# A transformer encoder layer on one core: the first sequence's output projection by seven products of block sums, in two halves of the depth, and its final norm beside the second sequence's products

## The chip, the cores and the metric

One core of one Trainium2 chip. The metric is the device time of one execution in microseconds, median of three runs. Engines: PE (TensorE, matmuls), PEld (its weight loads), DVE (VectorE), ACT (ScalarE), POOL (GpSimd) and SP (SyncE, which issues most DMAs).

## What is computed

One layer of a bidirectional encoder for a sample of 1024 tokens and a prompt of 512 tokens, D = 2048, in fp32, and a final norm:

```python
h = rms_norm(x, norm_g)
z = h @ w_in
c_val, c_glu, c_gate, q, k, v, a_gate = split(z)
conv_out = conformer_conv(c_val, c_glu, w_dw, b_dw, ln_g, ln_b, w_pw) * silu(c_gate)
attn_out = banded_sink_attention(rope(q), rope(k), v, sink) * silu(a_gate)
y = rms_norm(x + concat([conv_out, attn_out]) @ w_out, final_norm_g)
```

`conformer_conv` is a gated unit, a depthwise convolution of 31 taps, a layer norm over 1024 channels, a silu and a product with `w_pw` (1024 x 1024). The attention has 8 heads of 128 in two groups, in bands of blocks of 128 tokens. `w_out` is 2048 x 2048: its first 1024 rows meet the convolution half of the mix, its last 1024 the attention half. Weights are the same for both sequences.

## The kernel before

Every fp32 product is made as three products of parts: ACT copies a tile into its upper part (L379), DVE subtracts that from the tile and leaves the lower part (L380, `parts`), and PE multiplies upper by upper, upper by lower and lower by upper into one bank of PSUM. Matmuls have a 128x128 weight and 128x512 of tokens. Values lie channel by channel in partitions, tokens along the row; the first sequence has two halves of 512 tokens.

**Seven products.** The first sequence's input projection is made by units (`Unit`). A unit takes two columns of 128 outputs, the two halves of 512 tokens and 8 blocks of 128 of the depth (1024), and treats them as a 2x2 by 2x2 product of blocks: seven products of sums and differences of blocks instead of eight. Each is 4 blocks x 3 parts = 12 matmuls (L190), so a unit has 84. The weight differences are made on DVE from two raw tiles (L140, `make1` and `make2`), the sums of token blocks come from DRAM, where they were put earlier (`load_sum`, `token_sum`). `tap` (L216, L236) evacuates each product from PSUM and adds it to up to four results on ACT and DVE. The depth of 2048 takes two units; the first stores its part in DRAM, the second adds it by an accumulating DMA that POOL issues. Units of one half of the depth come one after the other; at the change to the other half (`switch`) the token sums are exchanged step by step.

**Jobs.** All other products are jobs (`Job`): one column of 128 outputs by 512 tokens. The prompt's input projection has jobs of 48 matmuls (L517), a job of `w_pw` 24, a job of `w_out` 48.

**Order of the work.** Python code emits everything in the order in which it shall run on PE; each engine runs its own rows in that order and waits for semaphores. First come the units of the first sequence's input projection (4 stages), then the prompt's jobs, then for each of three posts (the sample's two halves, `Post`, and the prompt, `LastPost`) eight `first_jobs` (with `w_pw`) and for the sample's halves sixteen `last_jobs` (with `w_out`), 2 x 16 x 48 matmuls in all. Beside these, lanes (`conv`, `attn`, `prep`) hand out side work step by step, as matmul time goes by (`tick`), at a rate set by `pace`: the convolution's taps, the attention, the norms. `until` forces a lane's steps out before the job that needs them. A post's layer norm (`prepare`) sums the channels on DVE (L1089, L1091) and over partitions on PE (L559), takes squares, the column sums (L548), a root, spreads it (L584) and makes the normed, silu'd tiles and their parts. The sample's second half has its norm beside the first half's `last_jobs` (it is started at `lj[1]`), and the prompt's beside the second half's. `project` adds the residual and gathers squares; `finish`, the final norm, scales 16 tiles of a half (L1192) and stores them.

**The end.** `last_run` makes the prompt's output projection with tokens in partitions: four blocks j of 512 output columns; in each, four accumulators (one for each 128 tokens) take 48 matmuls of 128x512 each (L1316). `rows_done` (L1287 and on) adds the residual rows (`x_p`), squares, and scales. `load_rows` (L1272, L1276) loads the final norm's gain and the rows of `x_p`, 512 KB each, ahead of the run. Accumulators alternate between two sets of four banks: a, b, a, c and s, s, pt, pv.

The functions that the change touches, and what calls them:

## Time and profile before

| | |
|---|---|
| median of three runs | 2159.8 us (2158.51 to 2161.04) |
| profiled execution, its own time | 2161.61 us |
| its span in the trace | 2159.8 us |
| granted TensorE clock, mean | 0.997 |
| PE busy | 2121.6 us, 98% |
| DVE busy | 1631.5 us, 76% |
| ACT busy | 1017.6 us, 47% |
| DMA | 400.13 MB, 185 GB/s |

A row of the trace's chain or timeline has the start in us from the span's start, the length, the engine, the source line (L517 is line 517 of the kernel before), and how often. In square brackets stands how long the engine was idle just before and what released it. A row of a group by line and form has `out<-in` by the program's names, the shape and type of both, the count, then busy us, mean ns of one, and the idle time before these with its releasers. A row of the windows has the stretch, its length, the busy time of PE, PEld, DVE, ACT and POOL with counts, the granted clock, the DMA share and GB/s.

### The profile page before, as it was taken

What the parts mean: (1) busy time and instruction counts of PE and PEld (TensorE: products, weight loads), DVE (VectorE), ACT (ScalarE), POOL (GpSimd) and SP (SyncE); (2) the same over time, 40 slices, a digit from 0 to 9 for tenths busy, and PEclk for the clock granted to TensorE, in tenths of its full rate; (3) what the DMA queues carried; (4) which work ended last, traced back from release to release, by engine and by line L of the source; (5) the groups of instructions that cost most, each with busy time, mean ns of one, the idle gap of its engine ahead of it and who ended that gap; (6) DMA issues with size and microseconds to landing.
All of it is one profiled execution on the core that took longest, in us unless ns stands there. A gap on an engine that the chain in (4) does not pass through costs nothing.

```text
span 2159.8 us, 26503 instructions
## 1 busy us (share of the span) xinstructions
PE 2121.6 (98%) x9510; PEld 1747.2 (81%) x9510; DVE 1631.5 (76%) x2493; ACT 1017.6 (47%) x1620; POOL 77.4 (4%) x92
## 2 busy tenths in 40 slices
PE   8999999999989999899999999999999999999998
PEld 5887888888878888688888888888888888888886
DVE  8657799988889999899887669986675467446343
ACT  6475445333544444544464656745574325232232
POOL 0001110000011111000000000000000000000000
PEclk9999999999999999999999999999999999999999
DMA  8978878754766767754446444564534493438342
GB/s 276 324 255 248 227 179 272 267 181 156 234 189 176 185 156 203 236 179 161 138 142 225 131 138 137 166 216 154 190 122 135 152 316 110 150 113 268 97 128 78
DMA packets 208037, 400.13 MB, mean 185 GB/s; under 512 B 18976, under 2 KB 76704, under 8 KB 207904
## 3 DMA queue, kind: packets, MB, share of 16 engines
q1 hardware_dynamic: 195232, 375.36, 52.5%
q0 software_dynamic: 12672, 23.07, 6.6%
q8 instruction: 74, 1.21, 0.2%
q14 instruction: 59, 0.48, 0.1%
HBM read 294.02 MB, written 104.33 MB: 184 GB/s over the span
## 4 chain that ended last, share of the span: by engine, by line
PE 79%; issue 9%; DVE 5%; DMA 3%; ACT 2%; POOL 2%; SPq 0%; POOLq 0%; ACTq 0%; DVEq 0%
PE a L517 21%; PE a L190 13%; PE c L517 11%; PE b L517 10%; PE c L190 6%; PE b L190 3%; PE s L971 2%; PE pv L1000 2%; PE a L1316 2%; PE s L1316 2%; PE pt L1005 1%; PE b L1316 1%; PE c L1316 1%; PE pv L1316 1%; PE pt L1316 1%
## 5 line engine op out<-in xcount | busy, mean ns | idle before, releaser
L379 ACT ACTIVATE hl<-raw 128x1024 fp32r<-128x1024 f32 (+1 forms) x332 | 312.8, 943 | 509.8 <-issue 109.0
L380 DVE TENSOR_TENSOR hl<-raw,hl 128x1024 fp32r<-128x1024 f32 (+1 forms) x332 | 357.7, 1078 | 250.9 <-ACT hl L379 246.0
L517 PE MATMUL a<-t,hl 128*128 128x512 f32 x2112 | 505.7, 392 | 1.2 <-DVE hl L380 1.2
L190 PE MATMUL a<-t,hl 128*128 128x512 f32 x1968 | 475.6, 392 | 13.7 <-ACT t L382 7.5
L517 PEld LDWEIGHTS a<-t,hl 128*128 128x128 f32 x2112 | 392.7, 188 | 81.6 <-DVE hl L380 1.7
L845 DVE SCALAR_TENSOR_TENSOR f<-f,c_w_dw,f 128x1024 f32<-128x1024 f32 (+1 forms) x464 | 454.2, 1013 | 3.6 <-ACT f L840 3.4
L190 PEld LDWEIGHTS a<-t,hl 128*128 128x128 f32 x1968 | 369.3, 189 | 96.7 <-ACT t L382 7.9
L517 PE MATMUL b<-t,hl 128*128 128x512 f32 x1056 | 253.9, 392 | 0.1
L517 PE MATMUL c<-t,hl 128*128 128x512 f32 x1056 | 253.2, 392 | 0.0
L190 PE MATMUL c<-t,hl 128*128 128x512 f32 x984 | 239.1, 390 | 3.1 <-ACT t L379 1.1
L517 PEld LDWEIGHTS b<-t,hl 128*128 128x128 f32 x1056 | 196.3, 188 | 40.3 <-DVE hl L380 0.6
L517 PEld LDWEIGHTS c<-t,hl 128*128 128x128 f32 x1056 | 196.6, 188 | 39.8
L190 PEld LDWEIGHTS c<-t,hl 128*128 128x128 f32 x984 | 184.4, 188 | 43.4 <-ACT t L379 2.2
L190 PE MATMUL b<-t,hl 128*128 128x512 f32 x492 | 118.6, 389 | 0.0
L190 PEld LDWEIGHTS b<-t,hl 128*128 128x128 f32 x492 | 92.3, 188 | 19.3
L216 ACT ACTIVATE g<-a 128x512 f32<-128x512 f32 x88 | 52.2, 593 | 67.2 <-PE a L190 60.6
L379 ACT ACTIVATE a<-pt 128x512 fp32r<-128x512 f32 x64 | 38.1, 596 | 79.1 <-PE pt L1005 78.9
L216 ACT ACTIVATE u<-a 128x512 f32<-128x512 f32 x76 | 45.3, 596 | 63.5 <-PE a L190 59.8
L1316 PE MATMUL a<-hl,t 128*128 128x512 f32 x192 | 74.7, 390 | 0.0
L985 ACT ACTIVATE p<-p,tiny 128x384 f32<-128x384 f32 (+1 forms) x96 | 54.6, 571 | 38.5 <-DVE tiny L982 30.1
L974 DVE CUSTOM_DVE_ANT_0 p<-s,c_mask,c_attn_sink 128x384 f32<-128x384 f32 (+1 forms) x96 | 51.2, 570 | 17.2 <-PE s L971 17.0
L380 DVE TENSOR_TENSOR a<-pt,a 128x512 fp32r<-128x512 f32 x64 | 44.0, 688 | 23.1 <-ACT a L379 22.4
(261 smaller groups left out, 2261.6 us busy)
## 6 DMA issues: line engine op xcount, KB each, us to landing
raw<-w_in SPq DMA_DIRECT2D x172, 512.0 KB, 4.7
raw<-w_out SPq DMA_DIRECT2D x64, 512.0 KB, 3.7
raw<-w_out SPq DMA_DIRECT2D x64, 256.0 KB, 3.3
raw<-w_pw SPq DMA_DIRECT2D x24, 512.0 KB, 3.5
f<-xT_s SPq DMA_DIRECT2D x38, 256.0 KB, 6.0
f<-x_s SPq DMA_DIRECT2D x16, 512.0 KB, 6.7
f<-x_p SPq DMA_DIRECT2D x13, 512.0 KB, 7.1
a<-sum_S SPq DMA_DIRECT2D x24, 256.0 KB, 3.8
```

Of the source, the lines that this page charges most:

```text
L190: nc.tensor.matmul(acc, hl[:, l, o, j, :], toks[j][:, r], start=name in FRESH and j == 0 and q == 0, stop=name in LAST and j == HALF - 1 a ...
L216: nc.scalar.activation(t, bank, AF.Copy)
L379: nc.scalar.activation(hi, x, AF.Copy)
L380: nc.vector.tensor_tensor(lo, x, hi.bitcast(F32), ALU.subtract)
L517: nc.tensor.matmul(job.acc[0], hl[:, l, kk // HALF, kk % HALF, :], r, start=i == 0 and p == 0, stop=i == nk - 1 and p == 2,)
L845: nc.vector.scalar_tensor_tensor(t, h[:, j : j + T], w(j), t, ALU.mult, ALU.add)
L971: nc.tensor.matmul(ps[:, 0:n], qs[:, x, h], k[y][:, keys], start=p == 0, stop=p == 2)
L974: nc.vector.tensor_tensor_reduce(p[:, 0:n], ps[:, 0:n], mask, SCALE, e.sink[:, g * GROUP + h : g * GROUP + h + 1], ALU.add, ALU.max, accum ...
L985: nc.scalar.activation(p[:, 0:n], p[:, 0:n], AF.Exp, bias=nm[:, h : h + 1], accum_out=l[:, h : h + 1])
L1000: nc.tensor.matmul(pv, v[x][:, vs], pt[:, y], start=i == 0 and p == 0, stop=i == last and p == 2)
L1005: nc.tensor.transpose(tp[:, h], p[:, i * P : (i + 1) * P], e.ident)
L1316: nc.tensor.matmul(acc, self.mix[self.KS[i]][:, m, b * P : (b + 1) * P], part[l].rearrange("p a b -> p (a b)"), start=i == 0 and p == 0, s ...
```

## The change

The lines of the changed kernel lie some lines lower: L190 becomes L192 (units), L517 L519 (jobs), L380 L382 (lower parts), L559 L561, L548 L550, L584 L586.

- The sample's output projection is no longer made by `last_jobs` but by units of the class `Mix`: 8 pairs of columns x 2 halves of the depth, so 16 units of 84 matmuls. First all units of the attention half of the depth (`over[0]`), whose parts are stored, then those of the convolution half (`over[1]`), which add the parts, then the residual (`project`), gather squares and store the unscaled result in `y_d`.
- The products of the two posts with `w_pw` now come one after the other: eight jobs of the first half of the tokens, eight of the second. The second half's layer norm starts at the first half's first job. The mixed tiles go to DRAM.
- Block sums of the mix (`block_sums`) are made on DVE by side work: those of the attention half beside the prompt's last jobs, those of the convolution half beside `over[0]`; the token sums of the attention half are loaded beside the second half's eight jobs (`fill`).
- The prompt's attention runs on as side work beside the posts and the units; its layer norm lies beside `over[1]`. Norms use additions of 128x1024 (two channels' tiles at once).
- The sample's final norm (`Mix.finish`) loads `y_d` again, scales whole tiles of 128x1024 (L1207) and stores them, beside the prompt's jobs with `w_pw` and its last run.
- `load_rows` is called inside the last run, in the middle of its first block j.

The core of the diff:

```diff
-    for n, post in enumerate(posts):
-        fj = post.first_jobs()
-        fj[0].before.insert(0, lambda post=post: until(lambda: len(post.cs) == NC, e.prep))
-        jobs += [[j] for j in fj]
-        if n + 1 < len(posts):
-            lj = post.last_jobs()
...
-            lj[1].before.append(lambda nx=posts[n + 1]: prepare(nx))
-            jobs += [[j] for j in lj]
+    for n, half in enumerate(halves):
+        fj = half.first_jobs()
+        fj[0].before.insert(0, lambda half=half: until(lambda: len(half.cs) == NC, e.prep))
+        pace(fj[0], LN_RATE if n == 0 else 1.0, e.prep)
+        if n == 0:
+            fj[0].before.append(lambda: e.prep.add(halves[1].prepare()))
...
+        jobs += [[j] for j in fj]
+    out = mix.units()
+    over = [[u(1, False) for u in out], [u(0, True) for u in out]]
...
+    switch(over[0][-1], over[1][0], 0, mix)
...
+    over[1][2].before.append(norm_last)
...
+    jobs += grouped(over[0], False) + grouped(over[1], True)
+
+    fj = last.first_jobs()
+    fj[0].before.append(lambda: e.prep.add(last.attention_parts()))
+    fj[1].before.append(lambda: e.prep.add(mix.finish()))
+    jobs += [[j] for j in fj]
...
-    for lane in e.lanes:
-        lane.drain()
-    posts[-1].load_rows()
-    posts[-1].last_run(at)
+    last.last_run(at)
```

```diff
+                    if j == 0 and i == ND // 2:
+                        for lane in e.lanes:
+                            lane.drain()
+                        self.load_rows()
```

In the rows below, a name with numbers is one tile of the program (`hl` weights' parts, `a`, `b`, `c`, `s`, `pt`, `pv` banks of PSUM, `t1` tiles of the norm and of tokens, `raw` weights as loaded).

PE around the spread of the layer norm of the sample's second half (L584, L586). Before, among the products of a job with `w_out` of the first half:

```order
L517 MATMUL a_1870_13024<-t1_1666_11811,hl_1860_12966 128x512 x3
L517 MATMUL a_1870_13024<-t1_1713_12114,hl_1871_13028 128x512 x3
L517 MATMUL a_1870_13024<-t1_1730_12178,hl_1871_13028 128x512 x3
L584 MATMUL s_1882_13094<-u_1883_13095,ones_r_192 128x512
L584 MATMUL s_1882_13094<-u_1884_13101,ones_r_192 128x512
L517 MATMUL a_1870_13024<-t1_1739_12233,hl_1871_13028 128x512 x3
L517 MATMUL a_1870_13024<-t1_1744_12275,hl_1871_13028 128x512 x3
```

Now, between attention blocks (L1007, L1002) ahead of the second half's first product with `w_pw` (`b_1789`):

```order
L586 MATMUL s_1761_12493<-u_1762_12494,ones_r_256 128x512
L1007 MATMUL pt_1773_12557<-c_ident_773,p_1745_12400 128x128
L1007 MATMUL pt_1773_12557<-c_ident_773,p_1747_12415 128x128
L586 MATMUL s_1761_12493<-u_1763_12500,ones_r_256 128x512
L1007 MATMUL pt_1773_12557<-c_ident_773,p_1749_12421 128x128
L1002 MATMUL pv_1772_12556<-a_1774_12562,f_1675_12009 128x512 x3
L1007 MATMUL pt_1783_12606<-c_ident_773,p_1743_12394 128x128
L1007 MATMUL pt_1783_12606<-c_ident_773,p_1745_12400 128x128
L1007 MATMUL pt_1783_12606<-c_ident_773,p_1747_12415 128x128
L1007 MATMUL pt_1783_12606<-c_ident_773,p_1749_12421 128x128
L1002 MATMUL pv_1772_12556<-a_1784_12611,f_1675_12009 128x512
L519 MATMUL b_1789_12656<-t1_1764_12512,hl_1781_12598 128x512
```

The norm's spread was followed by products that don't read it; now the next products read the tiles that it scales.

DVE where the same norm sums the channels. Before (the tile is `t1_1801`, the lines L1089 and L1091):

```order
L1089 TENSOR_TENSOR t1_1801_12598<-t1_1802_12599 128x512
L1091 TENSOR_TENSOR t1_1801_12598<-t1_1801_12598,t1_1803_12602 128x512
L380 TENSOR_TENSOR a_1794_12564<-pt_1793_12559,a_1794_12564 128x512
L1169 TENSOR_TENSOR f_1783_12485<-b_1784_12487,f_1783_12485 128x512
L380 TENSOR_TENSOR hl_1814_12654<-raw_1789_12533,hl_1814_12654 128x1024
L380 TENSOR_TENSOR a_1796_12584<-pt_1795_12579,a_1796_12584 128x512
L380 TENSOR_TENSOR a_1808_12632<-u_1759_12375,a_1808_12632 128x512
L1091 TENSOR_TENSOR t1_1801_12598<-t1_1801_12598,t1_1803_12602 128x512
L1091 TENSOR_TENSOR t1_1801_12598<-t1_1801_12598,t1_1804_12605 128x512 x2
L1091 TENSOR_TENSOR t1_1801_12598<-t1_1801_12598,t1_1805_12608 128x512 x2
L380 TENSOR_TENSOR hl_1826_12722<-raw_1799_12595,hl_1826_12722 128x1024
```

Now (the tile is `t1_1700`, the lines L1240 to L1244; L1287 evacuates the first half's jobs with `w_pw`, `a_1756` being the sixth and `c_1767` the seventh; L847 and L849 are taps of the prompt's convolution):

```order
L1287 TENSOR_TENSOR g_1755_12455<-a_1756_12457,g_1755_12455 128x512
L382 TENSOR_TENSOR hl_1781_12598<-raw_1758_12464,hl_1781_12598 128x1024
L847 SCALAR_TENSOR_TENSOR f_1667_11939<-f_1666_11932,c_w_dw_777,f_1667_11939 128x512
L1240 TENSOR_TENSOR t1_1700_12136<-t1_1701_12137,t1_1702_12140 128x1024
L849 TENSOR_TENSOR f_1667_11939<-f_1667_11939 128x512
L1242 TENSOR_TENSOR t1_1700_12136<-t1_1700_12136,t1_1703_12143 128x1024
L1287 TENSOR_TENSOR g_1766_12522<-c_1767_12524,g_1766_12522 128x512
L1242 TENSOR_TENSOR t1_1700_12136<-t1_1700_12136,t1_1704_12146 128x1024
L382 TENSOR_TENSOR hl_1790_12660<-raw_1769_12531,hl_1790_12660 128x1024
L1244 TENSOR_TENSOR t1_1700_12136<-t1_1700_12136 128x512
L382 TENSOR_TENSOR u_1722_12278<-t1_1700_12136,u_1721_12277 128x512
```

The additions stood among an attention block's parts and an evacuation of a job with `w_out` (L1169); they now stand among the evacuations of the first half's own jobs, behind that of the sixth.

SP where the last run's residual rows are loaded. Before, ahead of the run:

```order
L1272 DMA f_2301_16067<-final_gain 128x1024
L1276 DMA f_2302_16070<-x_p 128x1024
L1276 DMA f_2303_16071<-x_p 128x1024
L1234 DMA raw_2327_16149<-w_out 128x4x128 x2
L1276 DMA f_2304_16074<-x_p 128x1024
L1276 DMA f_2305_16075<-x_p 128x1024
L1234 DMA raw_2329_16179<-w_out 128x4x128 x2
L1276 DMA f_2306_16078<-x_p 128x1024
L1276 DMA a_2309_16083<-x_p 128x1024
```

Now, inside the run (`y_s` takes the sample's scaled results, `raw` the weights of the later blocks j):

```order
L375 DMA y_s<-f_2484_16696 128x1024
L1360 DMA raw_2535_17086<-w_out 128x4x128 x2
L1360 DMA raw_2546_17139<-w_out 128x4x128 x2
L1398 DMA f_2485_16702<-final_gain 128x1024
L1398 DMA f_2486_16703<-final_gain 128x1024
L1360 DMA raw_2548_17145<-w_out 128x4x128 x2
L1360 DMA raw_2551_17178<-w_out 128x4x128 x2
L1402 DMA f_2487_16706<-x_p 128x1024
L1360 DMA raw_2553_17184<-w_out 128x4x128 x2
L1360 DMA raw_2556_17217<-w_out 128x4x128 x2
L1402 DMA f_2488_16707<-x_p 128x1024
L1402 DMA f_2489_16710<-x_p 128x1024
```

The loads of `x_p` moved from ahead of the run's weights to behind those of its later blocks, and into other tiles (`f`), which the sample's final norm held before.

More of the change, by code (lines that the diff above doesn't have):

```diff
@@ L36 @@
 PM = 30
+LN_RATE = 1.6
 RUSH = 1.45
@@ L124, in load1 @@
         self.e.nc.sync.dma_start(self.r2, self.w[1])
-    first = False
+    first = late = False
     def make0(self):
@@ L712, in load_sum @@
         if wide:
-            pairs = [e.A([2, W], F32) for _ in range(HALF // 2)]
+            pairs = [(pool or e.A)([2, W], F32) for _ in range(HALF // 2)]
             tiles = [t[:, j] for t in pairs for j in range(2)]
@@ L1503, in encoder @@
     pace(pj[0], RATES[3])
-    pj[PM].before.append(lambda: prepare(posts[0]))
-    jobs = sum(items, []) + [[j] for j in pj]
     def until(fn, lane):
@@ new lines, in encoder, with fill @@
+    pj[PM].before.append(prepare)
+    jobs = sum(items, []) + [[j] for j in pj]
+    for n, half in enumerate(halves):
[4 more added lines that the diff above has]
+            fj[0].before.append(lambda: e.prep.add(halves[1].prepare()))
+        else:
+            def fill():
+                until(lambda: mix.gated == HALF, e.attn)
+                e.prep.add(mix.fill())
+            fj[0].before.append(fill)
+        jobs += [[j] for j in fj]
@@ new lines, in encoder, with rest, norm_last @@
+    out = mix.units()
+    over = [[u(1, False) for u in out], [u(0, True) for u in out]]
+    def rest():
+        e.prep.drain()
+        mix.put(4)
+    over[0][0].before.append(rest)
+    over[0][0].after[0] = [lambda: (mix.put(5), mix.load(6))]
+    over[0][0].after[1] = [lambda: e.prep.add(mix.conv_sums())]
+    over[0][0].after[3] = [lambda: mix.put(6)]
+    over[0][-1].before.append(e.prep.drain)
+    switch(over[0][-1], over[1][0], 0, mix)
+    def norm_last():
+        until(lambda: prompt.convolved == NC, e.conv)
+        e.attn.drain()
+        e.prep.add(last.prepare())
@@ L1520, in encoder @@
+    over[1][2].before.append(norm_last)
+    over[1][-1].before.append(e.prep.drain)
+    for step in range(2):
+        over[1][-1].after[step] = [lambda i=i: last.split(i) for i in range(4 * step, 4 * step + 4)]
+    jobs += grouped(over[0], False) + grouped(over[1], True)
[3 more added lines that the diff above has]
+    jobs += [[j] for j in fj]
     e.weights_setup(jobs)
     at = len(e.preps)
-    e.preps += posts[-1].last_weights()
+    e.preps += last.last_weights()
@@ L1523, in encoder @@
     e.run(jobs)
-    for lane in e.lanes:
-        lane.drain()
-    posts[-1].load_rows()
-    posts[-1].last_run(at)
+    until(lambda: all(NC + h in last.mix for h in range(HEADS)), e.prep)
+    last.last_run(at)
 def kernel(**inputs):
```

326 lines of the change are left out of this document (210 added, 116 removed).

## The prediction

> **What bounds the kernel now.** I read the page first, for the engine that sets the span; its totals, its busy slices for PE and DVE, and the shares of the chain that ended last:
>
> ```profile
> span 2159.8 us, 26503 instructions
> PE 2121.6 (98%) x9510; PEld 1747.2 (81%) x9510; DVE 1631.5 (76%) x2493; ACT 1017.6 (47%) x1620; POOL 77.4 (4%) x92
> PE   8999999999989999899999999999999999999998
> DVE  8657799988889999899887669986675467446343
> PE 79%; issue 9%; DVE 5%; DMA 3%; ACT 2%; POOL 2%; SPq 0%; POOLq 0%; ACTq 0%; DVEq 0%
> ```
>
> PE is busy nearly everywhere and carries the chain. A matmul's end is modelled, so I asked the windows of the trace whether "busy" hides waits. The columns are the stretch, its length, then the busy time of PE, PEld, DVE, ACT and POOL, the granted clock, the DMA share and GB/s:
>
> ```profile
> 400.00:870.00 470.00, 461.30 (x2028) 379.22 (x2027) 433.29 (x559) 208.59 (x316) 46.48 (x53) 1.00 0.68 195
> 870.00:910.00 40.00, 34.57 (x151) 27.06 (x151) 33.55 (x49) 19.46 (x29) 2.63 (x3) 1.00 0.82 256
> 1450.00:1989.00 539.00, 538.88 (x2457) 447.45 (x2458) 328.53 (x547) 233.28 (x373) 0.00 (x0) 1.00 0.51 171
> ```
>
> From 1450 to 1989, which holds the whole first-sequence output projection, PE stands still for 0.12 us, and DVE has work for 328.5 of 539. So there every matmul that goes is worth its full pace, as long as nothing new makes PE wait. The chain of waits gives that pace, a product of old kind (L517, 48 matmuls) and the same product of the next unit in the seven-product scheme that the input projection already uses (L190):
>
> ```profile
> 73.46 5.44 PE a L190 x24
> 92.50 5.44 PE a L190 x24
> 1407.20 10.88 PE b L517 x48
> ```
>
> 10.88 / 48 = 0.2267 us a matmul in both, and a unit of seven products takes 92.50 - 73.46 = 19.04 us = 84 x 0.2267. The unit form itself costs PE nothing extra.
>
> **The change part by part.** *The product.* Before: 2 halves x 16 columns x 48 = 1536 matmuls. Now 8 pairs of columns x 2 halves of the depth x 7 products x 12 = 1344. 192 x 0.2267 = **-43.5 us**. The Trainium skill ("TensorE: Matmul & The Clock Gate", section "Wait — 56ns, not 53.3ns?") gives 215.7 ns for such a matmul on the full clock; the trace has 226.7, and by the page's figure the gain would be 41.4 us.
>
> *What pays for it on the other engines.* Block sums of both halves of the depth, weight differences, token sums and seven evacuations a unit: by the program's order DVE has 134 more 128x512 additions, 9 more of 128x1024, 16 more 128x1024 scalings and 32 fewer of 128x512; ACT has 152 more passes of 512 and 32 fewer of 1024; SP issues 136 more DMAs, and POOL 32 more that add (it is busy for 4%, and nothing waits there for long). Durations, by line and form:
>
> ```profile
> L380 DVE TENSOR_TENSOR hl<-raw,hl 128x1024 fp32r<-128x1024 f32 x242 | 296.1, 1224 | 242.5 <-ACT hl L379 237.7 <-DMA raw<-w_out 4.2 <-ACT f L1174 0.3
> L845 DVE SCALAR_TENSOR_TENSOR f<-f,c_w_dw,f 128x1024 f32<-128x1024 f32 x232 | 292.4, 1280 | 1.5 <-ACT f L840 1.3
> L845 DVE SCALAR_TENSOR_TENSOR f<-f,c_w_dw,f 128x512 f32<-128x512 f32 x232 | 161.8, 746 | 2.1 <-ACT f L840 2.1
> L1101 DVE TENSOR_TENSOR t<-t 128x512 f32<-128x512 f32 x21 | 14.4, 687 | 3.0 <-ACT t L1099 3.0
> L974 DVE CUSTOM_DVE_ANT_0 p<-s,c_mask,c_attn_sink 128x384 f32<-128x384 f32 x64 | 36.9, 614 | 11.1 <-PE s L971 10.9
> L583 DVE TENSOR_SCALAR u<-c_ident,tiny 128x128 fp32r<-128x128 f32 x32 | 7.1, 282 | 0.0
> L379 ACT ACTIVATE hl<-raw 128x1024 fp32r<-128x1024 f32 x242 | 256.0, 1058 | 363.3 <-issue 88.6 <-PE a L517 80.2 <-PE b L517 51.9
> L379 ACT ACTIVATE t<-u 128x512 fp32r<-128x512 f32 x50 | 30.6, 623 | 19.8 <-DVE u L1140 8.4 <-DMA u<-v_d 6.2 <-PE s L971 2.7
> L1114 ACT ACTIVATE u<-t,c_conv_ln_b,c_conv_ln_g 128x512 f32<-128x512 f32 x24 | 18.7, 808 | 5.6 <-DVE t L1112 5.6
> L565 ACT ACT_TABLE_LOAD x6 | 7.7, 1283 | 0.1
> 1974.17 0.96 SPq L1276 DMA_DIRECT2D f<-x_p  x2
> ```
>
> DVE: 134 x 0.687 + 9 x 1.224 + 16 x 1.280 - 32 x 0.746 = about 100 us, so some 1730 of 2120; ACT 152 x 0.62 - 32 x 1.06 = 60 us; SP 136 x 0.48 = 65 us. As totals these fit under PE. They cost where a stage has no room, and there are three such places.
>
> *Place 1: the layer norm of the second half of the first sequence.* Before, it lay beside 16 output jobs (16 x 10.88 = 174 us) and PE never waited for it. Now the second half's eight products follow the first half's eight at once, and the order puts the norm's first sum on DVE (L1240) only behind the evacuation of the sixth product (g_1755). I walk from T, the end of that product on PE. DVE: that evacuation 0.69, weights 1.22, a tap 0.75, four additions of 1024 or 512 (1.22, 0.69, 1.22, 1.22), evacuation 0.69, weights 1.22, a half addition 0.69: T+9.6. ACT's upper part 0.62, DVE's lower part 0.69: T+10.9; the sum on PE and the mean's copy on ACT, 0.45 and 0.60 plus two handovers: T+12.6. Then four centrings of 1.22, seven additions of squares of 0.69, four scores' passes of 0.70, one evacuation, one set of weights and some small ones: 14.4, T+27.0. Column sums, the square root's table 1.28 and seven small operations: T+30; eight diagonals of 0.28: T+32.3; spread and copy: T+33.5; the factor 1.22 and handover: T+34.9; silu 0.81 with its table in part: T+36.3; the two parts 0.62 and 0.69: T+37.6. Only now can the second half's first product start. PE has until then the seventh and eighth products (2 x 5.44), sums 0.90, twelve score matmuls of 0.17, column sums and what is left of an attention block: about 15.9 us. So it stands still for 37.6 - 15.9 = **21.7 us**. Behind it, two products are fed at the rate at which parts are made: eight times ACT's 0.81 + 0.62 = 11.4 us against 2 x 5.44 of PE, about 1 us more.
>
> A hole of such length has a second price, which the trace shows behind one of the kernel's longest waits:
>
> ```profile
> 614.51 4.58 PE L190 MATMUL pt<-t,hl 128*128 128x512 f32 x12 [4.93 <-ACT hl L379]
> 621.68 2.56 PE L190 MATMUL a<-t,hl 128*128 128x512 f32 x10
> 614.00:616.00 2.00, 1.49 (x3) 0.93 (x4) 2.00 (x4) 1.40 (x2) 0.00 (x0) 0.56 0.46 117
> 616.00:618.00 2.00, 2.00 (x6) 1.54 (x6) 2.00 (x4) 0.00 (x0) 0.00 (x0) 0.59 0.45 176
> 618.00:620.00 2.00, 1.08 (x5) 0.56 (x3) 2.00 (x4) 0.17 (x1) 0.00 (x0) 1.00 0.55 172
> ```
>
> After 4.93 us of waiting the granted clock is 0.56 and 0.59 for two windows, and twelve matmuls take 4.58 instead of 12 x 0.2267 = 2.72: +1.9 us. I add it once here: 21.7 + 1.0 + 1.9 = **+24.6 us**. Bounds: 0, if DVE should find its LN work done early as before; 34, if DVE comes to T late by a dozen taps of 0.75 that are queued ahead. The Trainium skill (same page, section "What's actually happening") says that the clock falls to half after one idle window of about 3.4 us and needs as long a busy one to return. The trace agrees with 4.93 us waited and about 3.5 us slow; the rule speaks against this change, as both this hole and the next are longer than its window.
>
> *Place 2: the second sequence's last run.* Its residual rows (x_p) and gains were loaded before the run started; now their loads come inside it, behind the scaled results of the first sequence and behind weight loads that wait for places that DVE frees. So the first rows are asked for at about the end E of the first two column blocks. Landing:
>
> ```profile
> f<-x_p SPq DMA_DIRECT2D x13, 512.0 KB, 7.1
> DMA to landing us min/median/max: 6.0/7.7/8.7
> ```
>
> In before these were issued from 1974 on, about where the run starts, and a first block of columns lasts 192 x 0.2267 = 43.5 us before they are added. Now: issue 0.5 to 1, landing 7.1 to 8.7, addition 0.69: PE's buffer is free at E+9.5. PE has 24 matmuls that need no such buffer, 24 x 0.2267 = 5.4, so it waits 4.1; three more buffers follow from rows that are issued 1 us apart, +1 to 2; the slow clock after it at most 1.9. Taken: **+7 us**; bounds 0 (rows asked for 10 us earlier) and 14 (each of the four buffers waits for its own landing).
>
> *Place 3: the sixteen new units.* Beside five of those of the convolution half lies the last norm: by the order DVE has 104 additions of 512, 21 of 1024 and eight diagonals: 104 x 0.687 + 21 x 1.22 + 8 x 0.28 = 99.3, with small ones 100.6 us, and PE 5 x 19.04 + 1 = 96.3. Weights made ahead take up part; +3.5. The switch from one half of the depth to the other is taken at 1.5, after the short wait at such a switch below:
>
> ```profile
> 186.00:400.00 214.00, 213.88 (x941) 176.34 (x942) 182.91 (x255) 101.24 (x156) 28.08 (x32) 1.00 0.79 220
> 620.51 0.73 PE L190 MATMUL a<-t,hl 128*128 128x512 f32 x2 [1.42 <-ACT hl L379]
> ```
>
> Taken **+5 us**. The first of these rows is the lower bound: with DVE at 183 of 214 the same units lost PE 0.1 us, so 0; the upper is 16, one us a unit, after 400 to 870, where DVE at 433 of 470 went with 8.7 us lost by PE over some 25 units' time, and more with DVE over PE's time.
>
> Sum: -43.5 + 24.6 + 7 + 5 = -6.9. The profiled execution took 2161.6 (1.8 beside its span); so 2154.7 there, and by the median, which lies 1.8 lower, **2153 us**. What a measurement of this kernel can tell from no change is about 0.2%, 4.3 us: 2155.5 and 2164.1 are the borders.
>
> **The rivals.** *A: the norm's hole alone.* The last run's loads land in time and the units run like 186 to 400 above. -43.5 + 24.6 = -18.9: 2141. For it: 538.88 of 539; against: the order of the loads behind weights.
>
> *B: the gain whole.* DVE has 200 us free in 1450 to 1989; if the norm's steps slip into earlier gaps, only 0 to 5 remains: about 2118. Against: the order is fixed, and L1240 stands behind g_1755.
>
> *C: slower, by DVE in the new units.* One mechanism: in units where DVE's work passes PE's, each of seven products waits for its evacuation and for its weights. It decides from DVE at 19.04 us a unit; I count 20 for the five with the norm, and the plain ones of the convolution half have 17.5 to 18. At 16 units x 1.2 us = 19 on top of the two other places: -43.5 + 24.6 + 7 + 19 + 2 (switch) = +9: 2169; with the norm's upper bound 2178. For it: 33.55 of 40 on DVE and 34.57 on PE from 870 to 910, where such units begin a sequence and PE loses 5.4 in 40. Against: 186 to 400.
>
> *D: the fewer matmuls don't shorten the chain*, since DMA paces it (share 0.82 from 870 to 910). Then the holes stand alone: 2190. Against: share 0.51 from 1450 to 1989.
>
> **How the numbers follow.** Forecast 0.55, its own range 2144 to 2163 (the terms at 17 to 30, 3 to 11 and 2 to 9, not all at one end); A 0.18; B 0.06; C 0.18; D 0.03. Of the forecast's 0.55, 0.34 lies under 2155.5, 0.17 between the borders and 0.04 above. Faster: 0.34 + 0.18 + 0.06 = 0.58; same 0.17 + 0.01 from C's lower end = 0.18; slower 0.04 + 0.17 + 0.03 = 0.24. The range takes in A and most of C, and leaves out B, D and C's upper end, under 0.2 together: 2132 to 2172.
>
> **What would show it.** In the profile after: nearly 192 fewer matmuls; one idle stretch of PE of about 20 us (in pieces, released by DVE or ACT parts of the norm) between the first and the second half's eight products, with the clock under 0.7 just after; in the last run one wait of 4 to 6 us some 5 us after the first 384 matmuls, released by DVE's addition of x_p; units that step by 19.04 to 20 us. I am wrong if the second half's products start without a wait over 10 us (A's or B's side), if DVE is busy over 97% through the convolution half and units step by over 20 us (C), or if the last run starts with its rows in place.

## The result, and the profile after

The changed kernel takes 2196.9 us (median of four, 2193.4 to 2199.1), against 2160.4 for before: ratio 1.0164, 95% interval 1.0141 to 1.0187. It is slower by 36.5 us, where 7 less were forecast. The profiled execution took 2199.1 us. The page after, by the same lines as before (totals, slices of PE and DVE and the clock, chain by engine):

```profile
span 2197.3 us, 26811 instructions
PE 2108.5 (96%) x9318; PEld 1728.0 (79%) x9318; DVE 1718.8 (78%) x2620; ACT 1070.5 (49%) x1742; POOL 105.0 (5%) x124
PE   7999999999989999999999999977999999898998
DVE  8657898988989999899987679768775578676543
PEclk9999999999999999999999999988999999998999
PE 68%; issue 14%; DMA 7%; DVE 6%; ACT 2%; POOL 2%; SPq 0%; POOLq 0%; ACTq 0%; DVEq 0%
```

192 instructions fewer on PE (9510 to 9318), but PE's busy time fell by 13 only, not by 43.5, and its share of the span by two hundredths: it stands still more, and it runs slower when it runs. The chain's share in DMA went from 3% to 7%. DVE's total is 1718.8, close to the 1730 that were worked out. The windows of the places, with the columns as in the prediction:

```profile
1450.00:1500.00 50.00, 37.22 (x153) 29.37 (x152) 36.82 (x63) 17.49 (x29) 0.00 (x0) 0.86 0.87 304
1500.00:1550.00 50.00, 33.97 (x131) 25.95 (x132) 41.17 (x72) 26.23 (x46) 0.00 (x0) 0.76 0.45 149
1550.00:1800.00 250.00, 249.28 (x1146) 206.09 (x1145) 171.49 (x302) 149.07 (x277) 1.73 (x2) 1.00 0.62 207
1800.00:1950.00 150.00, 139.09 (x589) 112.72 (x587) 115.95 (x177) 78.97 (x124) 25.26 (x29) 0.97 0.80 219
1950.00:2050.00 100.00, 90.59 (x386) 74.11 (x385) 58.56 (x94) 29.27 (x39) 0.86 (x1) 0.93 0.73 236
```

To put a number on each place I add, over windows of 2 us, PE's idle time and its busy time x (1 - granted clock), the time that the slow clock takes. The sums (idle + slow clock, us):

| stretch | what runs there | before | after | foreseen |
|---|---|---|---|---|
| 0 to 1450 | as before | 28.2 + 3.1 | 25.6 + 7.5 | |
| 1450 to 1500 | end of the prompt's jobs, first half's products | 0.1 + 0 | 12.8 + 3.8 | 0 |
| 1500 to 1550 | second half's norm | 0 | 16.0 + 6.4 | 24.6 |
| 1550 to 1800 | units of the attention half | 0 | 0.7 + 0 | } 5 |
| 1800 to 1950 | units of the convolution half | 0 | 10.9 + 4.8 | } |
| 1950 to 2050 | start of the last run | 0 | 9.4 + 4.5 | 0 |
| 2050 to the end | last run and tail | 9.9 + 0 | 13.4 + 2.8 | 9.9 + 7 |
| sum | | 38.2 + 3.1 | 88.8 + 29.8 | |

The losses rise by 118.6 - 41.3 = 77.3; 77.3 - 43.5 = 33.8, of the 37.5 by which the spans differ. The other 3.7 is work: PE's busy time less the slow clock fell from 2118.5 to 2078.7, by 39.8 and not by 43.5. Nearly half of the 77 was foreseen in place and size; most of the rest lies at places where nothing was foreseen, and 11 at the units, where too little was. Of the 77, 27 are the slow clock. PE's timeline at these places (in brackets the idle time just before, and what released it):

```profile
1465.53 7.75 PE L519 MATMUL a<-t,hl 128*128 128x512 f32 x24 [8.39 <-DVE f L794]
1476.38 7.34 PE L519 MATMUL c<-t,hl 128*128 128x512 f32 x24 [3.10 <-ACT g L856]
1531.18 1.87 PE L550 MATMUL s<-ones,t 128*128 128x1 f32 x8 [10.83 <-DVE t L1255]
1818.88 3.04 PE L192 MATMUL a<-t,hl 128*128 128x512 f32 x12 [1.48 <-ACT g L218]
1879.46 1.82 PE L550 MATMUL s<-ones,f 128*128 128x1 f32 x8 [2.14 <-DVE f L1255]
1903.11 7.31 PE L192 MATMUL a<-t,hl 128*128 128x512 f32 x24 [4.24 <-ACT g L218]
2000.26 0.79 PE L1442 MATMUL a<-hl,t 128*128 128x512 f32 x1 [7.52 <-DVE g L1287]
2102.57 7.03 PE L1442 MATMUL a<-hl,t 128*128 128x512 f32 x18 [3.43 <-DVE f L1413]
```

Twenty-four matmuls take 5.44 at full clock. After waits of 3.1, 4.2 and 8.4 us they take 7.3 to 7.8. The releasers are evacuations and additions on DVE and ACT, so the next question is what DVE had been waiting for. DVE's own list of waits, by line and releaser (total, times, longest), has what before's did not have among its longest:

```profile
DVE f L1106 <- DMA f<-ag_d: 19.8, 7, 6.7
DVE f L1207 <- DMA f<-y_d: 14.1, 8, 2.8
DVE g L1167 <- DMA g<-part_out: 12.4, 3, 5.7
DVE u L1347 <- DMA u<-ag_d: 8.7, 3, 7.8
DVE f L1413 <- DMA f<-x_p: 7.7, 3, 4.3
```

And the rows of DVE's timeline at three of the five, with the evacuation that stands behind (in the second case it is on ACT):

```profile
1463.53 1.23 DVE L1106 TENSOR_TENSOR f<-f,f 128x1024 f32<-128x1024 f32 x1 [4.04 <-DMA f<-ag_d]
...
1464.71 0.67 DVE L794 TENSOR_TENSOR f<-a,g 128x512 f32<-128x512 f32 x1
...
1899.81 0.69 DVE L1167 TENSOR_TENSOR g<-g,p 128x512 f32<-128x512 f32 x1 [5.74 <-DMA g<-part_out]
1900.53 0.63 ACT L1174 ACTIVATE p<-g 128x512 f32<-128x512 f32 x1 [4.85 <-DVE g L1167]
...
1902.48 0.57 ACT L218 ACTIVATE g<-a 128x512 f32<-128x512 f32 x1
...
1996.58 0.69 DVE L1347 TENSOR_TENSOR u<-u,u 128x512 f32<-128x512 f32 x1 [7.81 <-DMA u<-ag_d]
...
1999.52 0.68 DVE L1287 TENSOR_TENSOR g<-a,g 128x512 f32<-128x512 f32 x1
```

The last row, an evacuation of the last product 3 us behind the multiplication that waited (its releaser in PE's row at 2000.26), let the last run start. DVE runs its rows in a fixed order, and so does ACT. A multiplication or addition whose load is late (L1106, the gating for the block sums; L1167, the residual's addition behind POOL's accumulating transfer; L1347, the gating for the last run) holds up the evacuation that PE needs, though that evacuation depends on none of these loads. At 1900 this goes by way of ACT: its square (L1174) reads what L1167 adds, and the evacuation (L218) that lets PE go on at 1903.11 stands behind the square.

### The profile page after: what moved, and what is told of

The parts are those of the page before. It is cut to its first block, busy times and chain, and to the rows that moved or that the text cites. A ratio compares the mean times of both kernels' runs of the same rounds, so it can differ in the third digit from the quotient of the medians.

```text
span 2197.3 us, 26811 instructions
## 1 busy us (share of the span) xinstructions
PE 2108.5 (96%) x9318; PEld 1728.0 (79%) x9318; DVE 1718.8 (78%) x2620; ACT 1070.5 (49%) x1742; POOL 105.0 (5%) x124
## 4 chain that ended last, share of the span: by engine, by line
PE 68%; issue 14%; DMA 7%; DVE 6%; ACT 2%; POOL 2%; SPq 0%; POOLq 0%; ACTq 0%; DVEq 0%
PE a L192 17%; PE a L519 11%; PE c L192 9%; PE c L519 6%; PE b L519 6%; PE b L192 4%; PE a L1442 2%; PE pv L1002 2%; PE s L973 2%; PE s L1442 1%; PE s L192 1%; PE pt L1007 1%; POOL g L372 1%; POOL u L372 1%; DVE hl L382 1%
## 5 line engine op out<-in xcount | busy, mean ns | idle before, releaser
L192 PE MATMUL a<-t,hl 128*128 128x512 f32 x2688 | 654.3, 394 | 19.3 <-ACT g L218 8.0
L192 PEld LDWEIGHTS a<-t,hl 128*128 128x128 f32 x2688 | 506.7, 189 | 132.7 <-ACT g L218 11.7
L381 ACT ACTIVATE hl<-raw 128x1024 fp32r<-128x1024 f32 (+1 forms) x331 | 297.0, 899 | 399.2 <-DVE raw L142 67.3
L382 DVE TENSOR_TENSOR hl<-raw,hl 128x1024 fp32r<-128x1024 f32 (+1 forms) x331 | 339.4, 1026 | 188.8 <-ACT hl L381 188.1
L847 DVE SCALAR_TENSOR_TENSOR f<-f,c_w_dw,f 128x1024 f32<-128x1024 f32 (+1 forms) x464 | 454.1, 1014 | 4.5 <-ACT f L842 4.3
L519 PE MATMUL a<-t,hl 128*128 128x512 f32 x1344 | 331.1, 396 | 9.6 <-DVE f L794 8.4
L192 PE MATMUL c<-t,hl 128*128 128x512 f32 x1344 | 329.1, 391 | 2.7 <-DVE t L382 1.5
L519 PEld LDWEIGHTS a<-t,hl 128*128 128x128 f32 x1344 | 251.7, 190 | 60.8 <-issue 8.8
L192 PEld LDWEIGHTS c<-t,hl 128*128 128x128 f32 x1344 | 253.4, 189 | 57.0 <-DVE t L382 2.2
L519 PE MATMUL b<-t,hl 128*128 128x512 f32 x672 | 166.9, 395 | 2.0 <-ACT hl L381 1.1
L519 PE MATMUL c<-t,hl 128*128 128x512 f32 x672 | 163.5, 395 | 3.1 <-ACT g L856 3.1
L192 PE MATMUL b<-t,hl 128*128 128x512 f32 x672 | 163.8, 391 | 0.0
L519 PEld LDWEIGHTS c<-t,hl 128*128 128x128 f32 x672 | 126.1, 190 | 29.1 <-ACT g L856 3.5
L519 PEld LDWEIGHTS b<-t,hl 128*128 128x128 f32 x672 | 125.3, 189 | 28.7 <-DVE hl L382 1.8
L192 PEld LDWEIGHTS b<-t,hl 128*128 128x128 f32 x672 | 126.3, 188 | 26.1
L218 ACT ACTIVATE g<-a 128x512 f32<-128x512 f32 x120 | 71.3, 594 | 95.6 <-PE a L192 84.8
L218 ACT ACTIVATE u<-a 128x512 f32<-128x512 f32 x104 | 61.9, 595 | 85.7 <-PE a L192 76.9
L381 ACT ACTIVATE a<-pt 128x512 fp32r<-128x512 f32 x64 | 38.1, 595 | 77.5 <-PE pt L1007 77.3
L976 DVE CUSTOM_DVE_ANT_0 p<-s,c_mask,c_attn_sink 128x384 f32<-128x384 f32 (+1 forms) x96 | 51.4, 570 | 15.7 <-PE s L973 15.3
L382 DVE TENSOR_TENSOR a<-pt,a 128x512 fp32r<-128x512 f32 x64 | 44.0, 688 | 21.6 <-ACT a L381 21.2
```

Of the source, the lines that this page charges most:

```text
L192: nc.tensor.matmul(acc, hl[:, l, o, j, :], toks[j][:, r], start=name in FRESH and j == 0 and q == 0, stop=name in LAST and j == HALF - 1 a ...
L218: nc.scalar.activation(t, bank, AF.Copy)
L381: nc.scalar.activation(hi, x, AF.Copy)
L382: nc.vector.tensor_tensor(lo, x, hi.bitcast(F32), ALU.subtract)
L519: nc.tensor.matmul(job.acc[0], hl[:, l, kk // HALF, kk % HALF, :], r, start=i == 0 and p == 0, stop=i == nk - 1 and p == 2,)
L847: nc.vector.scalar_tensor_tensor(t, h[:, j : j + T], w(j), t, ALU.mult, ALU.add)
```

## The experiments

Theory W: the places that weren't foreseen are DVE waiting for transfers, at rows that the change added, ahead of evacuations. Rival L: DVE and ACT simply have too much work there, as rival C of the prediction had it. Theory N: the norm's chain makes the hole of 1500 to 1550. Edits are to the changed kernel. Most of the variants have one time each, and the four of the changed kernel spread over 6 us, so there the stretches tell more than the times; each loss below is idle + slow clock as in the table.

**Block sums later.** The gap between the loads and the multiplication of the attention half's block sums is doubled.

```diff
-            yield 2 * LOAD
+            yield 4 * LOAD
```

> Edit: the attention half's block sums leave twice as much time between the loads of a pair of tiles and the multiplication that reads them, so that on DVE the first product's evacuations stand ahead of these multiplications. Theory W (DVE runs its rows in a fixed order and sits on multiplications whose loads are still on the way; PE then waits for the evacuation queued behind): the two waits of 8.4 and 3.1 us at 1465 to 1477 and the slow clock after them go, some 10 to 15 us of the 16 lost between 1450 and 1500; the time is 2182 to 2188. Rival L (DVE and ACT have too much work there): the waits only move, time 2193 to 2199.

Measured 2191.5. The wait of 8.4 ahead of 1465 is gone and the one behind it is 1.6:

```profile
1470.09 5.74 PE L519 MATMUL a<-t,hl 128*128 128x512 f32 x24 [1.63 <-ACT g L856]
```

The norm starts earlier with it: 1450 to 1550 loses 29.9 instead of 39.0. But 1450 to 1500 itself still loses 12.7 of its 16.6, where 1 to 6 were expected to stay: PE now waits 5.8 us at the norm's first sums (L561), whose upper part on ACT waits for a buffer that a block sum is still being stored from.

```profile
1491.77 0.63 ACT L381 ACTIVATE u<-t 128x512 fp32r<-128x512 f32 x1 [3.98 <-DMA msum_S<-u]
```

And 1800 to 1950 loses 20.6 instead of 15.7, so only 5 us come out at the end, between what W and what the rival expected: W for the wait at 1465, and a gain that was largely handed on.

**Results read later.** The step that reads the accumulated result stands six turns behind, not four.

```diff
-            e.later.append([LANDING, self.done(n[0], n[1], d)])
+            e.later.append([6 if self.late else LANDING, self.done(n[0], n[1], d)])
```

> Edit: in the new units, the step that reads a result after POOL's accumulating transfer comes six products' half steps after its issue instead of four. Theory W: DVE no longer sits up to 5.7 us on results that are on the way (the transfers took 8.7 us there), and of the 15 us that PE loses between 1800 and 1950 some 8 to 12 go: 2184 to 2189. Rival L (DVE has 100.6 us of work for 96.4 us of PE in five of these units): the loss stays over 12 us, 2194 to 2199. A rival B: results held longer starve the evacuations of buffers, and the loss grows: over 2199.

Measured 2190.9. 1800 to 1950 loses 9.2 instead of 15.7, and no row of DVE waits for these transfers there any more. DVE's load was a little higher (119.4 of 150 us, for 115.9); W, under the 8 to 12 expected.

**Attention tiles two heads ahead,** for the last run, every second head in another set of buffers:

```diff
-                f, g = e.U(), e.U()
+                f, g = (e.PT("p", NP, [W]), e.PT("p", NP, [W])) if h % 2 else (e.U(), e.U())
...
         load(0)
+        load(1)
...
-            load(h + 1)
...
+            load(h + 2)
```

> Edit: the prompt's attention tiles for the last run are loaded two heads ahead into a second set of buffers, instead of one. Theory W: the wait of 7.5 us ahead of the last run and the slow clock behind it came from DVE sitting 7.8 us on the gate of the last head; both go, and most of the 14 us lost between 1950 and 2050: 2184 to 2189. Rival S (the loads wait in SP's order behind the loads of the first sequence's results): PE still waits 5 us or more ahead of the last run, 2193 to 2199.

Measured 2186.1. The loss of 13.9 between 1950 and 2050 is gone whole:

```profile
1950.00:2050.00 100.00, 100.00 (x450) 82.77 (x449) 66.37 (x101) 31.82 (x41) 0.00 (x0) 1.00 0.85 279
```

So PE's wait hung on the load of the last head's gate (`ag_d`). The run doesn't tell the buffers from SP's order, rival S: in the changed kernel the last gate's load is issued at 1988.1, behind three loads of results (`y_d`), and with the edit at 1976.3, ahead of these. But the run without accumulation below keeps the order (1966.3, behind three) and loses nothing here, so the order alone doesn't make the wait.

**Rows early.** The first halves of three of the four blocks of `x_p` rows are loaded ahead of the last run into free buffers.

```diff
+        if early:
+            self.rows = [[e.A([half], F32) if b < 3 else None, None] for b in range(NB)]
+            for b in range(3):
+                load(b, 0)
+            return
...
+    last.load_rows(True)
     last.last_run(at)
```

> Edit: the residual rows of three of the four blocks of tokens that the first column blocks need go into buffers that are free ahead of the last run and are loaded there; the fourth and the second halves stay where they are. Theory: the wait of 3.4 us at the third column block with its slow clock, 6 us in all between 2050 and 2150, falls to 0 to 3: 2191 to 2195. Rival: the wait has another source (weights), and stays as it is: 2195 to 2199.

Measured 2191.2. The wait didn't shrink, it moved, to the one block whose row still came late (4.13 us, accumulator c, released by the addition of that row):

```profile
2091.25 0.50 PE L1449 MATMUL c<-hl,t 128*128 128x512 f32 x1 [4.13 <-DVE f L1420]
```

So the rows do set it, and one late row of four costs about as much as four. The time lies in the range of the theory by luck: from 2050 on 15.7 are lost for 16.2, and the rest of the gain stands at places that the edit doesn't touch (13.5 for 15.7 from 1800 to 1950, 9.4 for 13.9 from 1950 to 2050). In the five edits below all four are early, and this wait is gone.

**The half's norm left out.** Mean, variance and scaling of the second half's layer norm are left out; loads, silu and parts stay.

```diff
+        if t0:
+            for i, t in enumerate(pairs):
...
+                    self.normed(n, t[:, j])
+            return
```

> Edit: the layer norm of the first sequence's second half of tokens leaves out its mean, variance and scaling (part of the computation is left out; the loads, the silu and the parts stay), to price the hole between the two sets of eight products. Theory N (the chain of dependent steps from the first sum to the first part makes the hole, 37.8 us after the sixth product with 16 us of PE work in it): the 22 us lost between 1500 and 1550 fall to under 5, time 2176 to 2182. Rival (loads and evacuations set it, and the norm only fills the time): over 12 us stay lost, 2187 to 2199.

Measured 2169.2, 27.8 less, and more than either expected. PE isn't idle at all there:

```profile
1500.00:1550.00 50.00, 50.00 (x234) 40.81 (x234) 38.45 (x70) 30.91 (x61) 0.00 (x0) 1.00 0.78 252
```

N: the 22.4 us of loss hang on the chain. The other 5 lie elsewhere, among it 12 matmuls of the norm fewer and 4.3 less lost before 1450, where nothing was changed.

**The norm's side work at 4.0.** `LN_RATE` from 1.6 to 4.0.

> Edit: the layer norm's side work is handed out at 4.0 of matmul time instead of 1.6 beside the first half's eight products; on DVE its first sum moves from behind the sixth evacuation to behind the fifth, and the centrings stand together. Theory N: the hole shrinks by as much as the chain starts earlier, 3 to 7 us: 2190 to 2195. Rival (DVE is late there with older work, so the order doesn't matter): within 2 us of the changed kernel, 2195 to 2200.

Measured 2198.8: nothing. 1500 to 1550 loses 22.0 instead of 22.4. The time is the rival's, its reason isn't: DVE does the norm's first sum (L1240) at 1505.3 instead of 1508.7, and the second half's first product starts at 1539.2 instead of 1543.3. But PE waits as long as before for the column sums:

```profile
1528.45 1.86 PE L550 MATMUL s<-ones,t 128*128 128x1 f32 x8 [10.69 <-DVE t L1255]
```

Twelve score matmuls of the attention (L973) that ran before this wait (1516 to 1520) now stand behind the spread (1534 to 1539), so the chain came earlier with less work beside it. In the five edits below, which have this edit and the later block sums, 1450 to 1550 loses 18.6, where the block sums alone left 29.9; no run has just the two.

**No accumulation.** The units of the convolution half leave out the accumulating transfers, and so the attention half's part of the result.

```diff
-            e.add_into(d, part)
+            if not self.late:
+                e.add_into(d, part)
```

> Edit: the units of the convolution half leave out the accumulating transfers that add the attention half's part (part of the computation is left out). Theory W (DVE sits on these transfers): the 15 us that PE loses between 1800 and 1950 fall under 6, and the wait ahead of the last run shrinks, since the first part of it came through the same transfers: 2180 to 2188. Rival L (DVE's load of 100.6 us for 96.4): over 10 us stay lost in the units, 2192 to 2199.

Measured 2170.6, less than either expected. DVE is busier than in the changed kernel and PE loses 3.7 instead of 15.7, and nothing between 1950 and 2050:

```profile
1800.00:1950.00 150.00, 147.94 (x646) 121.15 (x645) 130.75 (x198) 86.59 (x135) 0.00 (x0) 0.99 0.63 209
1950.00:2050.00 100.00, 100.00 (x449) 82.81 (x448) 58.15 (x86) 27.08 (x33) 0.00 (x0) 1.00 0.79 262
```

That is against L: DVE at 130.75 of 150 with a loss of 3.7, at 115.95 with one of 15.7. The run takes the transfers' traffic away too (DMA share 0.63 for 0.80); with the transfers kept, reading six turns behind is the nearer test. Without these transfers the start of the last run loses nothing either. In the changed kernel DVE waits for two of them (5.3 us at 1954, 3.0 at 1966) ahead of the last heads' rows; that these waits make the last gate's load late is an inference.

**Five edits together:** later block sums, results read six turns behind, attention two heads ahead, norm at 4.0, and the rows of all four blocks early.

> Edits together: later multiplications of the block sums, results read six steps after their accumulation, attention tiles two heads ahead, the norm at rate 4, and the residual rows of all four blocks of tokens for the first two column blocks in buffers that are loaded ahead of the last run. Theory: the places are separate, and the gains add: 8 (block sums) + 6 (accumulation) + 12 (attention) + 5 (rows) + 3 (norm) = 34 off the changed kernel, 2160 to 2168, about the time of before. Rival: a place that is relieved hands its traffic and DVE work to the next, as later block sums did, and half of it goes: 2175 to 2185.

Median 2166.0 of eight runs (2157.8 to 2167.8), before 2162.0 beside it: ratio 1.0017, interval 1.0004 to 1.0029. 31 us come off the changed kernel, of 34 added up; it is level with before to within 0.3%. Its profiled execution, 2160.0, is one of the two fastest. In it 78.6 are lost, 37 more than before, half of that (18.6) from 1450 to 1550: PE waits 11.5 us at the norm's column sums, which its order puts ahead of other products.

```profile
1499.45 1.87 PE L550 MATMUL s<-ones,t 128*128 128x1 f32 x8 [11.47 <-DVE t L1255]
```

**Room for the norm:** the five edits, the prompt's taps paused beside the first half's products, column sums one product later.

```diff
+        if n == 0:
+            pace(fj[0], 0.0)
...
-        yield S3
+        yield (4 if t0 else 1) * S3
         v = e.column_sums(va, N, 1.0 / C, LN_EPS)
```

> Edit: the five edits, and two that give the half's layer norm room: the prompt's convolution taps pause beside the first half's eight products, and the column sums of the norm stand on PE behind the seventh of them instead of the sixth (in the five edits PE waited 11.5 us at these column sums with two products of 5.4 us each queued behind). Theory N: of the 18 us lost between 1450 and 1530 6 to 10 go: 2150 to 2157, faster than before. Rival: the taps come back where DVE is needed in the convolution half, and the time stays at 2158 to 2166.

Ratio to before 1.0020 (1.0008 to 1.0031): no gain. The time is the rival's, but not through the convolution half (9.0 lost from 1800 to 1950, 8.6 with the five edits). The wait moved from the column sums to an evacuation that now stands behind the norm on DVE:

```profile
1497.94 0.79 PE L519 MATMUL c<-t,hl 128*128 128x512 f32 x1 [10.99 <-DVE g L1287]
```

**The same, results read seven turns behind.**

> Edit: as the run with room for the norm, and results of the convolution half's units read seven steps after their accumulating transfer instead of six. Theory W: two to four us of the 8 lost there go, 2148 to 2155. Rival B: buffers held longer make evacuations wait, and it is slower than with six.

2183.3, ratio 1.0105 (1.0088 to 1.0122): 18 us slower than with six. Rival B. 1800 to 1950 loses 23.5: ACT's evacuations now wait for buffers whose last store hasn't ended:

```profile
1816.96 0.60 ACT L218 ACTIVATE g<-c 128x512 f32<-128x512 f32 x1 [5.72 <-DMA y_d<-g]
1834.19 0.63 ACT L381 ACTIVATE u<-f 128x512 fp32r<-128x512 f32 x1 [4.39 <-DMA y_d<-u]
```

**Places cleared:** the five edits, with the half's norm and the accumulation left out as above.

> Edit: the five edits, and left out (part of the computation) the mean, variance and scaling of the second half's layer norm and the accumulating transfers of the convolution half's units. Theory: seven products are worth their 43.5 us, and only the waits at these places took them; with all of them cleared the loss of PE is near that of before, and the time is 2118 to 2130. Rival M (the unit form or the added transfers cost PE something outside these places): 2140 or more.

Measured 2144.5, in rival M's range. The losses are 59.4 + 8.3 = 67.7, 26.4 over before; 2159.8 - 43.5 + 26.4 = 2142.7, and the span is 2142.8. That it comes out to the tenth is in part luck, since the run also leaves out 12 matmuls of the norm (9306 for 9318). By PE's busy time less the slow clock the seven products bring 43.4 here, 39.8 in the changed kernel and 38.9 with the five edits: 39 to 40 where the whole computation is made. And not all places were cleared. Of the 26.4, 16.7 stand from 1450 to 1500, ahead of the units, so the units' form isn't where most of it lies. The wait there is a new one: an evacuation that multiplies by a gate, whose load is late; whether the added transfers make it late isn't shown.

```profile
1495.91 3.33 PE L520 MATMUL c<-t,hl 128*128 128x512 f32 x7 [12.51 <-DVE g L1296]
```
```profile
1495.07 0.69 DVE L1296 TENSOR_TENSOR g<-c,g 128x512 f32<-128x512 f32 x1 [6.38 <-DMA g<-gate_d]
```

**Norm by sums of squares:** the five edits, with the variance from sums of squares less the squared mean, so that no centring stands in the chain.

> Edit: the five edits, and the layer norms take their variance from sums of squares less the squared mean, so that no centring and no copy of the mean stands between the sums and the factor; one more spread and four subtractions of 1024 stand behind. Theory N (the hole is the chain's length): the chain from the first sum to the first part falls from some 37 us by 6 to 9, and the time to 2150 to 2158, under both kernels. Rival: DVE's place in the order behind evacuations, not the chain's length, sets it: 2158 to 2166 as with the five edits.

Ratio to before 1.0025 (1.0015 to 1.0034), as with the five edits, and about the rival's time (2166.6): PE again waits 11.8 us for an evacuation (the profiled execution is the slowest of the ten, so its stretches aren't set beside the others).

**Gates apart:** the five edits, the gates in buffers of their own (`p`), which the block sums don't use. **Gates and squares:** the same with sums of squares.

```diff
-        f = e.G()
+        f = e.G() if self.out is e.a["y_p"] else e.PT("p", NP, [W])
```

> Edit: the five edits, and the gates of the sixteen products with w_pw in buffers that the block sums don't use. Theory G (gates wait for buffers that hold block sums): PE's waits between 1450 and 1550 fall from 18.6 us lost to 8 to 13, time 2148 to 2156, faster than before. Theory N (the norm's chain sets the hole): 17 to 22 us stay lost there, 2158 to 2166.

> Edit: as the run with gates apart, and the norms by sums of squares. Theory G with N: both the gates and the chain's length show, 4 to 8 us under the run with gates apart. Rival: no further gain, within 3 us of it.

2180.4, ratio 1.0090 (1.0075 to 1.0105), and 2182.5, ratio 1.0091 (1.0074 to 1.0107): both worse than the five edits. As theory G had it, the waits between 1450 and 1500 fell, from 15.1 to 4.5; but the second half's first product starts at 1514.3 instead of 1514.6, and PE, through with the first half's products sooner, waits for it later: 1500 to 1550 loses 24.7 instead of 3.5. With squares it starts at 1511.1, 3 us earlier. And 1550 to 1800 loses 14.3: 5.8 around a second-half product at 1578 that waits for an evacuation whose gate is late again (`p<-gate_d`), 6.1 at the units' change of depth at 1790. Between the five edits and the gates apart, then, the norm's end sets when PE goes on, and what is done to the evacuations ahead of it shifts where PE waits. Both theories missed: 29.2 are lost from 1450 to 1550, where G had 8 to 13 and N 17 to 22.

No version that makes the whole computation beats before; the five edits come nearest.

## Why the prediction was wrong, point by point

**The product, -43.5: right to 4 us.** PE's busy time less the slow clock fell by 39.8, and the units between 1550 and 1800 lost 0.7 us in 250.

**The norm's hole, +24.6: right in place and mechanism, and in sum partly by luck.** T, the end of the sixth product, is at 1505.7, the second half's first product at 1543.3: 37.6 us, as worked out. Lost in 1500 to 1550: 22.4. But PE was idle for 16.0 of it, where 22.7 were worked out, and the slow clock took 6.4, where 1.9 was taken (PE ran at half clock also in the bits of work inside the hole); the two errors nearly cancel. Leaving the norm out takes the loss away.

**The last run's rows, +7: right.** A wait of 3.4 (4.1 worked out), released by the addition of `x_p`, and a slow clock after it: 6.3 in all. With all four rows early it is gone.

**The units, +5: wrong in size and in cause.** 16.4 were lost. I priced DVE's work against PE's time. DVE was busy for 77% there and waited for accumulating transfers: landing took up to 8.7 us at a DMA share of 0.8, where before's such transfers had a median near 5. Without them the loss is 3.7 at a higher load of DVE. Rival C has the sign, and was worked out to 2169, but its mechanism was this overload, and it did not happen. Rival D is nearest in time, 2190, and also by luck: it has the product's gain vanish, and the gain is there.

**The step that failed** is the sentence "As totals these fit under PE. They cost where a stage has no room, and there are three such places." The totals did fit. What was missing was to ask of every row that the change added on DVE which transfer it reads, and what stands behind it. Two places of which the prediction says nothing cost 16.6 (L1106, before the first half's products) and 13.9 us (L1347, before the last run); with the 11 too few at the units that is 42 of the 44 by which it missed. The block sums later took the wait of 8.4 away, the results later DVE's waits for the accumulating transfers (15.7 lost to 9.2), the attention ahead its place's whole loss (13.9 to 0). That POOL's transfers add "and nothing waits there for long" is the same error: nothing waits on POOL, DVE waits for what it sends.

**The slow clock** was counted at two places, 3.8 us; it took 26.7 more than before, 4.4 of that ahead of 1450, where nothing was changed. In the rows above it followed every wait of 3.1 us and more, so such a wait cost about 2 us beyond itself (24 matmuls took 7.3 to 7.8 for 5.44), and several make a term of their own. The Trainium skill's rule ("TensorE: Matmul & The Clock Gate", section "What's actually happening": half the clock after one idle window of about 3.4 us) agrees with the longer of these waits. But a wait's length alone doesn't settle it here. One of 1.96 us in the changed kernel was followed by a clock of 0.80, 0.50 and 0.85 (windows of 2 us from 868 on), and its 12 matmuls took 4.50 instead of 2.72:

```profile
868.01 4.50 PE L192 MATMUL a<-t,hl 128*128 128x512 f32 x12 [1.96 <-ACT g L218]
```

At the same place of the kernel before a wait of 1.88 left it at 1.00, and one of 3.40 did so in the run without the half's norm (18 matmuls at full pace are 4.08):

```profile
2072.42 4.37 PE L1450 MATMUL a<-hl,t 128*128 128x512 f32 x18 [3.40 <-DVE f L1421]
```

Open: what a form of the second half's norm would have to look like that leaves PE no hole. The runs show that neither its rate, nor its place among the evacuations, nor three us off its end does it; giving it other products as cover (an order in which units come between the two halves' products) was not tried.

## What to carry to other kernels

For every instruction that a change adds to an engine that evacuates for PE, write down the transfer that it reads, and what stands behind it in that engine's order: the engine's busy share says nothing about a wait at the head of its queue. Read the landing times where the transfers will run, not over the whole kernel, and leave as many steps as that takes, but no more buffers than there are. When a gain on PE is taken by waits, sum idle time and slow clock by stretch before and after; the ledger tells what was and wasn't foreseen, and whether the gain itself was real.

## What the runs showed of the hardware

After waits of 1.5 and 1.6 us that left the clock at 1.00 the next 12 or 24 matmuls took 0.3 us more than at full pace (3.04 for 2.72, 5.74 for 5.44); after 3.1 and 4.2 us, with the clock halved, 24 of them took 1.9 more (7.34 and 7.31). Between 1.88 and 3.40 us the runs have waits of both kinds. Behind the wait of 1.96 at 868 the loss of clock over the windows adds up to 3.4 us of half clock, (0.20 + 0.50 + 0.15) x 2 / 0.5, as it does behind the wait of 4.93 in the kernel before, (0.44 + 0.41) x 2 / 0.5.

On the chain that ended last, loads of 512 KB landed in 7.7 and 9.1 us, one of 256 KB in 8.5 and an accumulating one in 8.7, where the DMA share was 0.7 to 0.9; over the whole changed kernel the medians of the same transfers are 7.4, 5.2 and 5.6:

```profile
1439.06 9.08 DMA f<-ag_d
...
1945.66 8.66 DMA g<-part_out
...
1988.11 8.45 DMA u<-ag_d
```
